# A feed-forward stage whose first unit is done by plain products instead of seven block products

## The chip, the cores and the metric

The kernel runs on one core of one Trainium2 chip. What counts is the time of one execution in microseconds on the device. All times below are of that kind, and "us" is a microsecond. TensorE (PE in the profile) multiplies matrices, PEld is its loading of weights, VectorE (DVE), ScalarE (ACT) and GpSimd (POOL) work on tiles of 128 partitions, and SyncE (SP) issues most transfers. Each engine takes its instructions in the order of its own queue.

## The reference, cut to what matters

The network has three layers over 512 tokens of width 1024. The first has attention, a recurrent part and one feed-forward part, the other two have a feed-forward part, a mix of four attentions, and another feed-forward part. So there are five feed-forward stages, f0 to f4 below, in order of time. The first layer adds the whole product, the others half of it:

```python
def rms_norm(x, g):
    y = xf * lax.rsqrt(jnp.mean(xf * xf, axis=-1, keepdims=True) + EPS)
    return (y * g.astype(jnp.float32)).astype(x.dtype)

def swiglu(h, w_gate, w_up, w_down):
    return (jax.nn.silu(h @ w_gate) * (h @ w_up)) @ w_down
...
        x = x + 0.5 * swiglu(rms_norm(x, ffn1_norm[l]), ffn1_w_gate[l], ffn1_w_up[l], ffn1_w_down[l])
        h = rms_norm(x, mix_norm[l])
...
        x = x + 0.5 * swiglu(rms_norm(x, ffn2_norm[l]), ffn2_w_gate[l], ffn2_w_up[l], ffn2_w_down[l])
        x = rms_norm(x, final_norm[l])
```

The hidden width is 2816, eleven units of 256 gate and 256 up columns.

## The kernel before

Activations stand transposed: xT is 8 tiles (k) of 128 features by 512 tokens. Every fp32 operand is split into a high part and the rest (hi and lo, xh and xl, wh and wl), and every product is three matmuls: hi by hi, hi by lo, lo by hi. `feat` and `feat2` (L144 to L165) do this plainly, with weights that `stream` (L116) loads in two buffers ("raw") and splits (L133 on ScalarE, L135 on VectorE or GpSimd).

A unit of a feed-forward stage isn't done so. Its gate and up columns and the two halves of the tokens make a 2 by 2 scheme of blocks over even and odd k tiles, which takes seven products of sums of blocks instead of eight (`unit`, L620; `prod`, L584). A product is 24 matmuls of 128x256, so a unit has 168. The block sums of the weights are called factors. A0 to A3 are the four blocks of a unit's weights, loaded by `load` (L575). s1 = A2 + A3 is added by a transfer that GpSimd issues (L625), s2 and s4 by VectorE (L628, L660), s3 by ScalarE and a transfer (L626, L627). `prod` splits a factor into wh (ScalarE, L588) and wl (VectorE, L593, or ScalarE and a transfer, L590 and L591). The block sums of x are made once a stage by `combine` (L378): x is the scaled tile, t its differences, and the splits by L219 and L220 go to xh, xl, x3h and x3l. The first products of unit 0 need A0 and s1.

The norm's sum of squares runs beside it. For each k tile `norm_sq` (L227) squares on ScalarE (L231) and adds on GpSimd (L233) into acc; ahead of f3 `final_norm` (L735) adds two such sums, one on VectorE (L752), one on GpSimd (L762). Then `norm_r` reduces acc on TensorE (L203), VectorE makes nm (L194), GpSimd the power (L196), TensorE spreads it (L212), and ScalarE copies it to rB (L215). rB scales a unit's results after the products (`act`, L610); the products don't need it. At f3 eight scalings of xT follow (L780).

After the last product of a unit L668 adds it into c, then come SiLU, the multiply by up, a split into fh and fl, and every two units a share of the down product (`down`, L672), whose matmuls are plain ones of 128x512 (L150 to L152). Later units' products and these are laced together.

A scheduler puts the instructions in order ahead of time. Each has its place in the program as its priority, and `tc.high_priority(offset=n)` moves it n instructions ahead. Before, a factor and its split stand 3000 ahead and a load 6000, which is more than a unit's instructions, so those of units 0 and 1 stand ahead of the stage as far as buffers allow. A1 lies in the "raw" buffers, which live throughout; A0, A2 and A3 lie in the pool of the stage (`ph_f`), whose memory held other tiles before, so their loads wait for the last use of those. In unit 0 the first three products are cut in two ranges of k (L629), so that they can begin before the last pair of tiles is there.

Of the kernel before, what the change touches and what calls it, by code (L numbers as in the profile page):

```python
# [8 lines left out]
FT = mybir.dt.float32  # L9
# [9 lines left out]
T = 512  # L19
# [73 lines left out]
class Kern:  # L93
# [284 lines left out]
    def combine(self, k, xk, g, xc):  # L378
# [3 lines left out]
        p = k // 2  # L382
        if k % 2 == 0:
            xc["x"] = self.t4("x")
            if "hi" not in xc:
                xc["hi"], xc["lo"] = ((self.xp.tile([128, 4, 4, 256], FR, tag="x" + n, name="x" + n),
                                       self.x3.tile([128, 4, 3, 256], FR, tag="x3" + n, name="x3" + n)) for n in "hl")
        x = xc["x"]
        hi, lo = xc["hi"], xc["lo"]
        S.activation(x[:, 2 * (k % 2):2 * (k % 2) + 2], xk.rearrange("p (a b) -> p a b", a=2), AF.Copy, scale=g)  # L390
        if k % 2 == 0:
            self.split(hi[0][:, p, 0], lo[0][:, p, 0], x[:, 0])
            return
        self.split(hi[0][:, p, 1:3], lo[0][:, p, 1:3], x[:, 2:4])
# [5 lines left out]
        self.split(hi[0][:, p, 3], lo[0][:, p, 3], t[:, 0])  # L400
        self.split(hi[1][:, p], lo[1][:, p], t[:, 1:4])

    def norm_c(self, gname, g0):
# [3 lines left out]
        def tile_done(k):  # L407
            self.combine(k, xT[:, k], self.col(gname, g0 + k), xc)
            self.norm_sq(xT[:, k], k, acc)
# [146 lines left out]
    def ffn(self, f, half, norm):  # L556
# [6 lines left out]
        with tc.tile_pool(name="ph_f", bufs=1) as pf:  # L563
            self.pf = pf
            self.t4 = lambda n: pf.tile([128, 4, 256], FT, tag="c", name=n, bufs=3)
            xh, xl = ([lambda p, c=c, x=x: x[c // 4][:, p, c % 4] for c in range(7)] for x in self.xc)
# [4 lines left out]
            def load(u, i):  # L571
                pool, tag, n = (pf, "raw2", 3) if i % 3 == 0 else (pf, "S", 4) if i == 2 else (self.wp, "raw", 2)
                t = pool.tile([128, 2 * T], FT, tag=tag, name=f"A{i}", bufs=n)
                with tc.high_priority(offset=6000):
                    nc.sync.dma_start(t, I["w_gu"][f, u, i])  # L575
# [5 lines left out]
            def early():  # L581
                return tc.high_priority(offset=3000)

            def prod(x, c, ranges=((0, 4),), dma=False):  # L584

                h, o = (pf.tile([128, 2 * T], FR, tag=n, name=n, bufs=3) for n in ("wh", "wl"))
                with tc.high_priority(offset=3000):
# [8 lines left out]
                for a, b in ranges:  # L596
                    for i in range(2):
                        out = ps[:, i * 256:i * 256 + 256]
                        for p in range(a, b):
                            sl = slice((4 * i + p) * 128, (4 * i + p) * 128 + 128)  # L600
                            mm(out, h[:, sl], xh[c](p), start=i == 0 and p == 0, stop=False)  # L601
                            mm(out, h[:, sl], xl[c](p), start=False, stop=False)  # L602
                            mm(out, o[:, sl], xh[c](p), start=False, stop=i == 1 and p == 3)  # L603
                    yield
                return ps.rearrange("p (a b) -> p a b", a=2)

            def act(u, j, c):

                k = 2 * u + j
                V.tensor_mul(c, c, rT)  # L610
# [6 lines left out]
            def soon():  # L617
                return tc.high_priority(offset=1000)

            def unit(u):  # L620
# [8 lines left out]
                r = ((0, 3), (3, 4)) if u == 0 else ((0, 4),)  # L629
                heads = [prod(x, c, r) for x, c in ((a11, 0), (s1, 3), (s2, 4))]  # L630
                c1, c2 = (pf.tile([128, 2, 2, 256], FT, tag="c", name="c", bufs=3) for _ in range(2))
                if u == 0:
                    for g in heads:
                        next(g)
                ps = whole(heads[0])
# [3 lines left out]
                ps = whole(heads[1])  # L639
# [3 lines left out]
                ps = whole(heads[2])  # L643
# [4 lines left out]
                ps = whole(prod(a12, 1, dma=True))  # L648
# [3 lines left out]
                ps = whole(prod(s3, 5))  # L652
# [8 lines left out]
                ps = whole(prod(s4, 2))  # L661
# [4 lines left out]
                ps = whole(prod(a22, 6, dma=True))  # L666
# [40 lines left out]
            for u in range(11):  # L707
                if u % 2 == 0 and u:
# [26 lines left out]
    def final_norm(self, l):  # L735
# [11 lines left out]
        def tile_done(k):  # L747
# [13 lines left out]
            if k:  # L761
                G.tensor_tensor(acc2[0], acc2[0], sq, op=OP.add)  # L762
# [1241 lines left out]
```

## Time and profile before

| | |
|---|---|
| median of 3 runs | 3338.43 us (3334.64 to 3338.55) |
| profiled execution: its time | 3331.87 us |
| profiled execution: its span | 3330.1 us |
| mean granted clock of TensorE | 0.949 of full |
| busy: TensorE, VectorE, ScalarE, GpSimd | 91%, 67%, 53%, 39% of the span |

The span runs from the first to the last instruction of the profiled execution; its own time is 1.8 us longer. Shares are of the span. An engine that is busy nine tenths of the time over the whole can still stand idle in short stretches, so stretches are looked at one by one.

### The profile page before, as it was taken

The page shows a single profiled execution, that of the slowest core. Times are in us where ns is not written, and L with a number is a line of the kernel's source. Part 1 is how long each engine was busy: PE and PEld are TensorE (multiplying, and loading weights), DVE is VectorE, ACT ScalarE, POOL GpSimd, SP SyncE. Part 2 cuts the span into 40 slices and gives each one's busy share as a digit, 9 for nine tenths or more (in the row PEclk, how much of TensorE's full clock was granted, in tenths as well). Part 3 has the DMA queues.
Part 4 walks back from the last instruction along what each step waited for, and adds up shares of the span by engine and source line. Part 5 has one row for each costly group of instructions (what it writes and reads, how often), then busy time and mean ns, then how long its engine had stood idle before and what let it go on. Part 6 is the DMA issues. An engine that isn't in the chain of part 4 may idle for free. (4 is left out here: it accounts for less than half of the span.)

```text
span 3330.1 us, 50223 instructions
## 1 busy us (share of the span) xinstructions
PE 3020.4 (91%) x19249; PEld 2721.9 (82%) x19249; DVE 2216.2 (67%) x3447; ACT 1764.0 (53%) x3007; POOL 1291.1 (39%) x1139
## 2 busy tenths in 40 slices
PE   7999999979997899999895999958999998859998
PEld 6888778878996899998774899948999987658997
DVE  7577774566765667658675766666766578667665
ACT  4577773454544454457654545444544667545453
POOL 0466531122332323277732332223322877233322
PEclk9999999989998999999897999979999999979999
DMA  4311113466763766532213766436664321157662
GB/s 131 106 58 50 50 39 102 141 164 156 177 152 86 177 165 163 132 101 91 57 32 79 173 161 164 111 98 168 167 164 109 106 83 51 32 133 170 172 162 73
DMA packets 136984, 391.74 MB, mean 118 GB/s; under 512 B 30692, under 2 KB 40420, under 8 KB 136584
## 3 DMA queue, kind: packets, MB, share of 16 engines
q1 hardware_dynamic: 105064, 273.18, 26.5%
q0 software_dynamic: 31680, 115.36, 19.0%
q8 instruction: 151, 2.47, 0.3%
q14 instruction: 89, 0.73, 0.1%
HBM read 297.77 MB, written 6.80 MB: 91 GB/s over the span
## 5 line engine op out<-in xcount | busy, mean ns | idle before, releaser
L133 ACT ACTIVATE hi<-raw 128x512 fp32r<-128x512 f32 (+3 forms) x512 | 314.5, 620 | 470.1 <-PE ps_t L151 187.3
L135 DVE TENSOR_TENSOR lo<-raw,hi 128x512 fp32r<-128x512 f32 (+1 forms) x342 | 295.5, 868 | 156.4 <-ACT hi L133 152.4
L588 ACT ACTIVATE wh<-A 128x1024 fp32r<-128x1024 f32 x220 | 231.5, 1055 | 311.2 <-PE ps_mm L602 146.7
L591 POOL DMA_DIRECT2D wl<-A x110 | 97.7, 888 | 693.9 <-ACT wl L590 664.2
L151 PE MATMUL ps_t<-fl,hi 128*128 128x512 f32 x760 | 297.3, 391 | 0.0
L152 PE MATMUL ps_t<-fh,lo 128*128 128x512 f32 x760 | 295.7, 389 | 0.0
L150 PE MATMUL ps_t<-fh,hi 128*128 128x512 f32 x760 | 295.5, 393 | 0.0
L601 PE MATMUL ps_mm<-xh,wh 128*128 128x256 f32 x920 | 268.8, 292 | 28.6 <-ACT wh L588 28.6
L603 PE MATMUL ps_mm<-xh,wl 128*128 128x256 f32 x920 | 270.6, 294 | 26.1 <-DMA wl<-A 16.3
L601 PE MATMUL ps_s<-xh,wh 128*128 128x256 f32 x840 | 244.6, 291 | 25.5 <-ACT wh L588 25.5
L602 PE MATMUL ps_mm<-xl,wh 128*128 128x256 f32 x920 | 267.4, 291 | 0.0
L603 PE MATMUL ps_s<-xh,wl 128*128 128x256 f32 x840 | 246.4, 293 | 17.8 <-DMA wl<-A 12.3
L181 PE MATMUL ps_mm<-lo,xh 128*128 128x256 f32 (+1 forms) x896 | 257.6, 290 | 2.0 <-DVE lo L135 2.0
L182 PE MATMUL ps_mm<-hi,xl 128*128 128x256 f32 (+1 forms) x896 | 255.5, 288 | 4.1 <-DVE xl L238 4.1
L135 POOL TENSOR_TENSOR lo<-raw,hi 128x512 fp32r<-128x512 f32 (+2 forms) x170 | 231.9, 1372 | 65.3 <-ACT hi L133 61.3
L180 PE MATMUL ps_mm<-hi,xh 128*128 128x256 f32 (+1 forms) x896 | 256.1, 290 | 0.1
L612 POOL TENSOR_TENSOR c<-c 128x512 f32<-128x512 f32 x110 | 164.8, 1498 | 212.6 <-ACT c L611 212.5
L593 DVE TENSOR_TENSOR wl<-S,wh 128x1024 fp32r<-128x1024 f32 x165 | 208.8, 1266 | 55.9 <-ACT wh L588 55.4
L602 PE MATMUL ps_s<-xl,wh 128*128 128x256 f32 x840 | 243.6, 290 | 0.0
L588 ACT ACTIVATE wh<-S 128x1024 fp32r<-128x1024 f32 x165 | 174.2, 1056 | 73.3 <-PE ps_mm L602 40.8
L603 PE MATMUL ps_s<-x3h,wl 128*128 128x256 f32 x720 | 207.1, 288 | 6.4 <-DMA wl<-A 6.1
L601 PEld LDWEIGHTS ps_mm<-xh,wh 128*128 128x128 f32 x920 | 184.1, 200 | 32.7 <-ACT wh L588 30.5
(580 smaller groups left out, 9908.5 us busy)
## 6 DMA issues: line engine op xcount, KB each, us to landing
A<-in_w_gu SPq DMA_DIRECT2D x220, 512.0 KB
wl<-A POOLq DMA_DIRECT2D x110, 512.0 KB, 5.4
raw<-in_w_d SPq DMA_DIRECT2D x108, 512.0 KB
S<-in_w_gu POOLq DMA_DIRECT2D x55, 512.0 KB, 7.4
A<-A POOLq DMA_DIRECT2D x55, 512.0 KB, 4.6
raw<-in_w_o SPq DMA_DIRECT2D x24, 512.0 KB
raw<-in_w_c SPq DMA_DIRECT2D x16, 512.0 KB
raw<-in_w_m SPq DMA_DIRECT2D x16, 512.0 KB
```

The source lines that it names most:

```text
L133: nc.scalar.activation(hi[:, :c], x, AF.Copy)
L135: eng.tensor_tensor(lo[:, :c], x, hi[:, :c].bitcast(FT), op=OP.subtract)
L150: mm(ps, wh, mh(km), start=s, stop=False)
L151: mm(ps, wh, ml(km), start=False, stop=False)
L152: mm(ps, wl, mh(km), start=False, stop=e)
L180: mm(out[tb], h, wh, start=k == 0 and tb % 2 == 0, stop=False)
L181: mm(out[tb], h, wl, start=False, stop=False)
L182: mm(out[tb], o, wh, start=False, stop=k == K - 1 and tb % 2 == 1)
L588: S.activation(h, x, AF.Copy)
L601: mm(out, h[:, sl], xh[c](p), start=i == 0 and p == 0, stop=False)
L602: mm(out, h[:, sl], xl[c](p), start=False, stop=False)
L603: mm(out, o[:, sl], xh[c](p), start=False, stop=i == 1 and p == 3)
```

## The change

Five things change. Unit 0 of each stage is done by `first`: plain products of 8 k tiles, 2 column tiles, gate and up, three matmuls each, 96 matmuls of 128x512, from weights w_g0 and w_u0 that `stream` loads and splits; L631 multiplies each result by rB on leaving the accumulator. For it `combine` splits each xT tile as a whole (`norm_split`, L237 and L238), and the block sums keep four tiles t of their own, split in one go of 1024 columns. Factors and loads are moved ahead by `ahead` and twice that, which begins at 113 instructions for unit 1 and grows with the place in the stage up to 3000. The adds of squares in `norm_c` and the second sum of `final_norm` go from GpSimd to VectorE. And the tiles of x grow, for which the memory of GpSimd's transfer queue is set to 4096 bytes; the mix's boxes lie in the larger tile.

```diff
@@ -380,25 +380,23 @@
 
         V, S = self.nc.vector, self.nc.scalar
         p = k // 2
+        if not xc:
+            xc["hi"], xc["lo"] = ((self.xp.tile([128, 8, T], FR, tag="x" + n, name="x" + n),
+                                   self.x3.tile([128, 4, 4, 256], FR, tag="x3" + n, name="x3" + n)) for n in "hl")
         if k % 2 == 0:
             xc["x"] = self.t4("x")
-            if "hi" not in xc:
-                xc["hi"], xc["lo"] = ((self.xp.tile([128, 4, 4, 256], FR, tag="x" + n, name="x" + n),
-                                       self.x3.tile([128, 4, 3, 256], FR, tag="x3" + n, name="x3" + n)) for n in "hl")
         x = xc["x"]
         hi, lo = xc["hi"], xc["lo"]
+        self.norm_split(xk, k, g, hi[0], lo[0])
         S.activation(x[:, 2 * (k % 2):2 * (k % 2) + 2], xk.rearrange("p (a b) -> p a b", a=2), AF.Copy, scale=g)
         if k % 2 == 0:
-            self.split(hi[0][:, p, 0], lo[0][:, p, 0], x[:, 0])
             return
-        self.split(hi[0][:, p, 1:3], lo[0][:, p, 1:3], x[:, 2:4])
         t = self.t4("t")
         V.tensor_sub(t[:, 0], x[:, 1], x[:, 0])
         V.tensor_sub(t[:, 1], x[:, 3], t[:, 0])
         V.tensor_sub(t[:, 2], x[:, 3], x[:, 1])
         V.tensor_sub(t[:, 3], x[:, 2], t[:, 1])
-        self.split(hi[0][:, p, 3], lo[0][:, p, 3], t[:, 0])
-        self.split(hi[1][:, p], lo[1][:, p], t[:, 1:4])
+        self.split(hi[1][:, p], lo[1][:, p], t)
 
     def norm_c(self, gname, g0):
 
@@ -406,7 +404,7 @@
 
         def tile_done(k):
             self.combine(k, xT[:, k], self.col(gname, g0 + k), xc)
-            self.norm_sq(xT[:, k], k, acc)
+            self.norm_sq(xT[:, k], k, acc, self.nc.vector)
 
         def finish():
             self.xc = xc["hi"], xc["lo"]
@@ -563,7 +561,12 @@
         with tc.tile_pool(name="ph_f", bufs=1) as pf:
             self.pf = pf
             self.t4 = lambda n: pf.tile([128, 4, 256], FT, tag="c", name=n, bufs=3)
-            xh, xl = ([lambda p, c=c, x=x: x[c // 4][:, p, c % 4] for c in range(7)] for x in self.xc)
+            xs = [x[0] for x in self.xc]
+            xh, xl = ([lambda p, x=x: x[0][:, 2 * p, :256], lambda p, x=x: x[0][:, 2 * p + 1, :256],
+                       lambda p, x=x: x[0][:, 2 * p + 1, 256:]]
+                      + [lambda p, c=c, x=x: x[1][:, p, c] for c in range(4)] for x in self.xc)
+            ks = [(k, k) for k in range(8)]
+            ahead = [3000]
             rT = rB.rearrange("p (t b) -> p t b", t=2)[:, :, None, :].to_broadcast([128, 2, 2, 256])
             fh, fl = {}, {}
             nbank = [0]
@@ -571,7 +574,7 @@
             def load(u, i):
                 pool, tag, n = (pf, "raw2", 3) if i % 3 == 0 else (pf, "S", 4) if i == 2 else (self.wp, "raw", 2)
                 t = pool.tile([128, 2 * T], FT, tag=tag, name=f"A{i}", bufs=n)
-                with tc.high_priority(offset=6000):
+                with tc.high_priority(offset=2 * ahead[0]):
                     nc.sync.dma_start(t, I["w_gu"][f, u, i])
                 return t
 
@@ -579,12 +582,12 @@
                 return pf.tile([128, 2 * T], FT, tag="S", name="S", bufs=4)
 
             def early():
-                return tc.high_priority(offset=3000)
-
-            def prod(x, c, ranges=((0, 4),), dma=False):
+                return tc.high_priority(offset=ahead[0])
+
+            def prod(x, c, dma=False):
...
             def act(u, j, c):
 
                 k = 2 * u + j
-                V.tensor_mul(c, c, rT)
+                if u:
+                    V.tensor_mul(c, c, rT)
                 S.activation(c[:, :, 0], c[:, :, 0], AF.Silu)
                 G.tensor_tensor(c[:, :, 0], c[:, :, 0], c[:, :, 1], op=OP.mult)
                 h, o = (pf.tile([128, T], FR, tag=n, name=n, bufs=8) for n in ("fh", "fl"))
@@ -616,6 +618,19 @@
 
             def soon():
                 return tc.high_priority(offset=1000)
+
+            def ctile():
+                return pf.tile([128, 2, 2, 256], FT, tag="c", name="c", bufs=3)
+
+            def first():
+
+                c = [ctile() for _ in range(2)]
+                for i, n in enumerate(("w_g0", "w_u0")):
+                    ps = self.feat2(self.stream(I[n][f], 8, 256), ks, lambda k: xs[0][:, k], lambda k: xs[1][:, k])
+                    for m in range(2):
+                        V.tensor_mul(c[m][:, :, i], *(x.rearrange("p (a b) -> p a b", a=2) for x in (ps[m], rB)))
+                for m in range(2):
+                    act(0, m, c[m])
 
             def unit(u):
...
-                r = ((0, 3), (3, 4)) if u == 0 else ((0, 4),)
-                heads = [prod(x, c, r) for x, c in ((a11, 0), (s1, 3), (s2, 4))]
-                c1, c2 = (pf.tile([128, 2, 2, 256], FT, tag="c", name="c", bufs=3) for _ in range(2))
-                if u == 0:
-                    for g in heads:
-                        next(g)
-                ps = whole(heads[0])
+                c1, c2 = ctile(), ctile()
+                ps = prod(a11, 0)
                 with soon():
                     S.copy(c1[:, 0], ps)
                 yield
-                ps = whole(heads[1])
+                ps = prod(s1, 3)
...
             d = iter(())
-            for u in range(11):
-                if u % 2 == 0 and u:
+            first()
+            at = 130
+            for u in range(1, 11):
+                ahead[0] = min(3000, at * 7 // 8)
+                at += 215 if u == 1 else 330
+                if u % 2 == 0:
                     d = down(list(range(2 * u - 4, 2 * u + (0 if u < 10 else 2))), u == 10)
                 for i, _ in enumerate(unit(u)):
                     if i in ((2, 6) if u < 10 else (2,)):
...
             if k:
-                G.tensor_tensor(acc2[0], acc2[0], sq, op=OP.add)
+                V.tensor_add(acc2[0], acc2[0], sq)
...
-        x3 = [self.x3.tile([128, 6, T], FT, tag=n, name="box3") for n in ("x3h", "x3l")]
-        slots = {"P": [x3[0][:, i] for i in range(6)] + [x3[1][:, i] for i in range(2)],
+        x3 = [self.x3.tile([128, 8, T], FT, tag=n, name="box3") for n in ("x3h", "x3l")]
+        slots = {"P": [x3[0][:, i] for i in range(8)],
...
+    A["w_g0"], A["w_u0"] = (np.stack([blocks(f[i][:, :256], 256)[0] for f in ff]) for i in range(2))
...
-    nc = bacc.Bacc("TRN2", target_bir_lowering=False, num_devices=1)
+    nc = bacc.Bacc("TRN2", target_bir_lowering=False, num_devices=1, dynamic_dma_scratch_size=4096)
```

Three places show how the queues change, all at the start of f2. Rows are an instruction's line, what it does, tiles written and read, and shape. First TensorE before: the last plain matmuls of the mix (ps_mm from yhl), the reduction of acc, and unit 0's first product (xh by A0's wh).

```order
L150 MATMUL ps_mm<-yhl,hi 128x512
L151 MATMUL ps_mm<-yhl,hi 128x512
L152 MATMUL ps_mm<-yhl,lo 128x512
L203 MATMUL ps_n<-ones,acc 128x1 x4
L212 MATMUL ps_n<-ident,rt 128x128 x4
L601 MATMUL ps_s<-xh,wh 128x256
L602 MATMUL ps_s<-xl,wh 128x256
L603 MATMUL ps_s<-xh,wl 128x256
```

The same after, at the end of the 96 plain matmuls (xh and xl by hi and lo of w_g0 into ps_s and of w_u0 into ps_t), which begin straight behind the mix's last matmul. L603 to L605 are now unit 1's first product.

```order
L150 MATMUL ps_t<-xh,hi 128x512
L151 MATMUL ps_t<-xl,hi 128x512
L152 MATMUL ps_t<-xh,lo 128x512
L203 MATMUL ps_n<-ones,acc 128x1 x4
L212 MATMUL ps_n<-ident,rt 128x128 x4
L603 MATMUL ps_s<-xh,wh 128x256
L604 MATMUL ps_s<-xl,wh 128x256
L605 MATMUL ps_s<-xh,wl 128x256
```

So the reduction and all products moved behind the plain unit; in f0 and f1 the reduction stands after 42 of the 96. Next the loads on SyncE before, from the last weights of the mix on: A1 of units 0 and 1, then A0, A2, A3 of unit 0 and A0 of unit 1.

```order
L126 DMA raw<-in_w_o 128x1024 x7
L575 DMA A_18249<-in_w_gu 128x1024
L575 DMA A_18495<-in_w_gu 128x1024
L575 DMA A_18145<-in_w_gu 128x1024
L575 DMA A_18147<-in_w_gu 128x1024
L575 DMA A_18149<-in_w_gu 128x1024
L575 DMA A_18391<-in_w_gu 128x1024
```

And after: the plain unit's weights, A1 of unit 1, a first piece of the down weights, A1 of unit 2, and only then A0 (A_18103), A2 and A3 of unit 1.

```order
L126 DMA raw<-in_w_o 128x1024 x7
L126 DMA raw<-in_w_g 128x1024 x2
L126 DMA raw<-in_w_u 128x1024 x2
L578 DMA A_18207<-in_w_gu 128x1024
L126 DMA raw<-in_w_d 128x1024
L578 DMA A_18491<-in_w_gu 128x1024
L578 DMA A_18103<-in_w_gu 128x1024
L578 DMA A_18105<-in_w_gu 128x1024
L578 DMA A_18107<-in_w_gu 128x1024
```

Seven transfers now stand between the mix's weights and the load of A0 (the four of the plain unit among them) where two of A1 stood. Last VectorE after, at the end of the block sums: acc is the sum of squares, t and x3l the block sums and their split, nm the step that waits for L203, and L631 empties the plain unit.

```order
L233 TENSOR_TENSOR acc<-acc,sq 128x512
L135 TENSOR_TENSOR lo<-raw,hi 128x512
L398 TENSOR_TENSOR t<-x,t 128x256
L220 TENSOR_TENSOR x3l<-t,x3h 128x1024
L194 TENSOR_SCALAR nm<-ps_n 128x4
L220 TENSOR_TENSOR x3l<-t,x3h 128x1024
L631 TENSOR_TENSOR c<-ps_s,rB 128x2x256 x2
L631 TENSOR_TENSOR c<-ps_t,rB 128x2x256 x2
L596 TENSOR_TENSOR wl<-A_18103,wh 128x1024
```

Before, the last two x3l stood behind nm too, no L233 stood in this queue, and A0's split into wl followed at once.

## Rows read from the trace of the kernel before

**Rows 1.** The profile's page, part 1: engine, busy us (share of the span), instructions.
```profile
PE 3020.4 (91%) x19249; PEld 2721.9 (82%) x19249; DVE 2216.2 (67%) x3447; ACT 1764.0 (53%) x3007; POOL 1291.1 (39%) x1139
```

**Rows 2.** Windows ahead of f0, f2, sum of five: length, busy (count), clock.
```profile
667.00:679.30 12.30, 4.16 (x18) 3.57 (x17) 6.39 (x12) 5.47 (x10) 3.60 (x3) 0.63 0.28 108
...
1773.30:1806.60 33.30, 4.20 (x18) 3.59 (x17) 22.95 (x42) 16.41 (x31) 16.78 (x8) 0.54 0.12 39
...
sum 137.20, PE 24.74 PEld 21.48 DVE 91.04 ACT 62.92 POOL 53.64; mean PE 4.95 PEld 4.30 DVE 18.21 ACT 12.58 POOL 10.73
```

**Rows 3.** The waits in total: engine, line, released by; us, times, longest.
```profile
PE ps_n L203 <- POOL acc L233: 56.9, 4, 22.2
```

**Rows 4.** Timeline of TensorE at f2: start, us, line, tiles; idle before it.
```profile
1795.73 1.86 PE L203 MATMUL ps_n<-ones,acc 128*128 128x1 f32 x8 [22.21 <-POOL acc L233]
...
1806.57 0.58 PE L601 MATMUL ps_s<-xh,wh 128*128 128x256 f32 x1 [5.44 <-ACT wh L588]
```

**Rows 5.** Timeline of all engines at f2's start.
```profile
1776.91 2.69 POOL L233 TENSOR_TENSOR acc<-acc,sq 128x512 f32<-128x512 f32 x2 [0.72 <-ACT sq L231]
1777.00 1.48 DVE L220 TENSOR_TENSOR xl<-x,xh 128x256 fp32r<-128x256 f32 x1
...
1785.90 0.41 DVE L220 TENSOR_TENSOR xl<-t,xh 128x256 fp32r<-128x256 f32 x1
...
1800.57 0.96 DVE L220 TENSOR_TENSOR x3l<-t,x3h 128x768 fp32r<-128x768 f32 x1 [0.91 <-ACT x3h L219]
1801.16 0.59 ACT L215 COPY rB<-ps_n 128x512 f32<-128x512 f32 x1 [0.62 <-PE ps_n L212]
1801.61 1.75 SPq L575 DMA_DIRECT2D A<-in_w_gu  x4
```

**Rows 6.** Windows from unit 0's last L668 to unit 1's (f0, f2, f3, sum).
```profile
714.40:747.20 32.80, 28.47 (x204) 26.67 (x203) 22.24 (x22) 17.55 (x24) 10.81 (x9) 0.95 0.69 162
...
1847.70:1873.90 26.20, 22.86 (x167) 22.15 (x167) 17.09 (x19) 13.55 (x19) 8.66 (x9) 0.93 0.68 153
2252.80:2286.90 34.10, 28.65 (x204) 27.65 (x204) 21.90 (x22) 17.75 (x24) 10.74 (x9) 0.90 0.63 158
...
sum 141.60, PE 125.43 PEld 120.08 DVE 98.49 ACT 74.69 POOL 48.05; mean PE 25.09 PEld 24.02 DVE 19.70 ACT 14.94 POOL 9.61
```

**Rows 7.** Timeline of TensorE: 128x512 matmuls at full, then half clock.
```profile
1399.73 0.39 PE L150 MATMUL ps_t<-fh,hi 128*128 128x512 f32 x1
1399.96 0.39 PE L151 MATMUL ps_t<-fl,hi 128*128 128x512 f32 x1
...
1771.37 0.63 PE L150 MATMUL ps_mm<-yhl,hi 128*128 128x512 f32 x1
1771.80 0.63 PE L151 MATMUL ps_mm<-yhl,hi 128*128 128x512 f32 x1
```

**Rows 8.** Lines L238 and L233: durations min/median/max ns, first and last start.
```profile
L238 DVE SCALAR_TENSOR_TENSOR xl<-xT,cols,xh x16: 742/1410/1784, 1433.2 to 2595.3; 128x512 fp32r<-128x512 f32 x16
...
L233 POOL TENSOR_TENSOR acc<-acc,sq x42: 1261/1370/7467, 637.4 to 2930.3; 128x512 f32<-128x512 f32 x42
...
L233 DVE TENSOR_TENSOR acc<-acc,sq x7: 677/680/686, 11.0 to 20.8; 128x512 f32<-128x512 f32 x7
```

**Rows 9.** f3: TensorE's L203, and L575's loads between 2178 and 2283 us.
```profile
2196.24 1.87 PE L203 MATMUL ps_n<-ones,acc 128*128 128x1 f32 x8 [17.33 <-DVE acc L752]
...
L575 SPq DMA_DIRECT2D A<-in_w_gu x12: 327/328/516, 2213.2 to 2281.1; - x12
```

**Rows 10.** Windows of nine units of f0, and of the first mix stage.
```profile
768.00:1051.00 283.00, 280.97 (x1887) 260.19 (x1886) 195.66 (x221) 139.14 (x184) 85.01 (x68) 1.00 0.59 146
1400.00:1773.00 373.00, 344.91 (x2153) 304.42 (x2152) 248.85 (x484) 219.88 (x468) 225.46 (x209) 0.94 0.24 68
```

**Rows 11.** The page, part 6: GpSimd's transfers, KB, us from issue to landing.
```profile
wl<-A POOLq DMA_DIRECT2D x110, 512.0 KB, 5.4
```

More of the change, by code (lines that the diff above doesn't have):

```diff
@@ L581, in early @@
             def early():
-                return tc.high_priority(offset=3000)
-            def prod(x, c, ranges=((0, 4),), dma=False):
+                return tc.high_priority(offset=ahead[0])
+            def prod(x, c, dma=False):
                 h, o = (pf.tile([128, 2 * T], FR, tag=n, name=n, bufs=3) for n in ("wh", "wl"))
-                with tc.high_priority(offset=3000):
+                with early():
                     S.activation(h, x, AF.Copy)
@@ L595, in prod @@
                 ps = self.bank(("mm", "s")[nbank[0] % 2])
[L596 to L604, printed above, removed]
+                for i in range(2):
+                    out = ps[:, i * 256:i * 256 + 256]
+                    for p in range(4):
+                        sl = slice((4 * i + p) * 128, (4 * i + p) * 128 + 128)
+                        mm(out, h[:, sl], xh[c](p), start=i == 0 and p == 0, stop=False)
+                        mm(out, h[:, sl], xl[c](p), start=False, stop=False)
+                        mm(out, o[:, sl], xh[c](p), start=False, stop=i == 1 and p == 3)
                 return ps.rearrange("p (a b) -> p a b", a=2)
@@ L642, in unit @@
                 yield
-                ps = whole(heads[2])
+                ps = prod(s2, 4)
                 with soon():
@@ L647, in unit @@
                 a12 = load(u, 1)
-                ps = whole(prod(a12, 1, dma=True))
+                ps = prod(a12, 1, dma=True)
                 with soon():
@@ L651, in unit @@
                 yield
-                ps = whole(prod(s3, 5))
+                ps = prod(s3, 5)
                 with soon():
@@ L660, in unit @@
                     V.tensor_sub(s4, a12, s2)
-                ps = whole(prod(s4, 2))
+                ps = prod(s4, 2)
                 with soon():
@@ L665, in unit @@
                 yield
-                ps = whole(prod(a22, 6, dma=True))
+                ps = prod(a22, 6, dma=True)
                 with soon():
```

## The prediction

> **What bounds the kernel now.** I read the busy table first. TensorE is busy 91% of the 3330.1 us span [rows 1], so only a stretch in which it stands still has time to give. There are five such stretches, one ahead of each feed-forward stage (f0 to f4, in order of time). Cut into windows that run from the last plain matmul ahead of a stage to the first product of its unit 0 [rows 2], they are 137 us long together, from 12.3 us in f0 to 33 us and more in f2 to f4, and TensorE works 24.7 us of them. Its granted clock there is 0.63 in f0 and 0.54 in f2, so most of a window lies at the lower of its two levels (1.2 of 2.4 GHz). The list of waits gives the first reason: four times the reduction L203 waits for the adds of squares on GpSimd, 56.9 us in all [rows 3]. The timeline of f2 shows the queue [rows 4]: L203 starts 22.21 us after TensorE fell idle, L212 behind it, and the products behind both, as TensorE takes its instructions in order. But the sum is not the only late thing. In [rows 5] the last split into x3l starts at 1800.57; at 1801.61 the first load of A0 is issued, since the stage's buffers lie where earlier work ended only then; and the first product starts at 1806.57, five us after the issue. So two chains end together, and what the change is worth hangs on the second: when A0 is issued, and what follows it.
>
> What follows is slow too. I take as the end of a unit the add L668 that empties its last product: in f2 unit 0 ends at 1847.7, 46.1 us after A0's issue at 1801.6. From there to unit 1's end it takes 32.8 us in f0, 26.2 in f2, 34.1 in f3, and 141.6 us in the five stages together [rows 6].
>
> **The change, part by part.** *Unit 0 by plain products.* Seven products of 24 matmuls of 128x256 go, with their factors; 96 matmuls of 128x512 come. One of these follows the other by 0.23 us at full clock and 0.43 us at half [rows 7], so the new unit is 96 x 0.23 = 22 us, or 41 us at half clock. It needs no A0, only x and its own weights, which the load queue now has ahead of the stage's other loads. So it fills the wait in which TensorE stood. Unit 1 becomes the first unit that needs A0, and goes through what unit 0 goes through now: it ends as long after A0's issue as unit 0 did (f2: 46.1 us). If A0 is issued as before, unit 1 ends where unit 0 ended, and each stage gains the stretch between the two ends. That is the first term: **141.6 us**. The 22 us are no cost as long as they lie in that wait. In f0 and f3 the stretch holds 204 matmuls and not the 168 of one unit [rows 6], so 36/204 of 32.8 and of 34.1 us is other units' work, still to be done: **minus 11.8 us**.
>
> *A0's issue.* It waits for the last x3l (in f3 for the eight scalings L780). VectorE gains eight L238 splits of 0.74 us and seven adds of 0.68 us [rows 8], 10.7 us a stage. It loses the twelve small splits of x, some 6 us by the 0.41 us of a piece of 256 columns [rows 5], and its last splits grow from 768 to 1024 columns, some 1.2 us by width from 0.96 us. Net 5.9 us. GpSimd's adds go, and with them contention: such an add took 7467 ns once against 1261 at best [rows 8], and a split of 0.41 us took 1.48 us when an add ran beside it [rows 5]. That gives perhaps 4 us back in f2. More important is where things stand in the queue. In f2 and f4 the last x3l stands behind nm (L194) on VectorE, before and after; nm waits for L203, and TensorE now does that behind all 96 plain matmuls. By hand, the splits, adds and weight splits take VectorE to about 25 us behind the stage's start before the last add, the plain unit ends near there, and A0 goes out some 3 us later: about 4 us later than now, in both. In f3 A0 came 17 us after L203's start (2196.24 to 2213.2 us [rows 9]); L203 now follows a plain unit of 22 us that waits in part for the last k tiles, so about 26 us instead of 17.5, and A0 some 8.6 us later. In f1 I take 3 us, in f0 1 us, where L203 stands in the middle of the plain unit. Together **minus 20.6 us**. Bounds: 0 if the contention that goes pays for it all; 66 us if the plain unit runs at half clock in f2 to f4 (41 us, so 20 to 15 us more in each, 45 in all).
>
> A rule of the Trainium skill bears on this term ("SBUF — State Buffer", "Who interferes with whom"): a VectorE instruction with two SBUF inputs and a GpSimd instruction that reads SBUF exclude each other, and whichever issues first holds the port. By it, nothing contends at a stage's start any more, and the term would be nearer 10 than 20 us; the 1.48 us beside the 0.41 us agree. I keep 20, since the queue order decides in three of the stages.
>
> *New waits.* The four L631 that empty the plain unit (0.68 us each by the add in [rows 8]) need rB, which comes some 6 us after L203's start [rows 4, 5]. They stand on VectorE ahead of the split of A0's weights; the first product starts five us after A0's issue, so at most 2.7 us, in practice 1 to 2 us a stage: **minus 7 us**. Bounds 0 and 14. Behind them wait the third matmul of the first product, and SiLU of unit 0, which nobody needs before the first down product.
>
> *Smaller lead of the loads* (`ahead`). Later units take 31.4 us each (283 us for nine, TensorE busy 280.97 of it [rows 10]); with 168 products and a share of the down product they are full. The new lead is one unit's instructions at the start and 3000 at the end, so a factor is still made a unit ahead: nothing, unless a load comes late, bound 1 us a unit. *The mix stages.* Their code is the same, but the order inside differs: 281 of the 1991 rows on TensorE stand elsewhere. TensorE idles 28 us in the first of them [rows 10]. I take 0, bounds plus and minus 12.
>
> **Sum.** 141.6 - 11.8 - 20.6 - 7 = 102 us. The profiled execution took 3331.87 us (1.8 us beyond its span), so 3229.7; the median of the three runs is 6.6 us above it, which makes **3236 us**.
>
> **Rivals.** (a) *Half clock.* In f2 to f4 the plain unit is fed k tile by k tile, one each 2 to 3 us, while its gate half needs 6 x 0.23 = 1.4 us for a tile. If the clock stays at 1.2 GHz through it, it takes 41 us, ends near 42 us instead of 25, and L203, x3l and A0 come that much later: 45 us lost, about 3281 us. For it speaks that the clock falls in these windows now [rows 2]; against it, that plain work follows the matmuls before it with hardly a gap and is dense once the up half joins. The Trainium skill ("TensorE: Matmul & The Clock Gate", "HAM oscillation — how this bites in real kernels") says that an engine fed in bursts with waits between them is throttled anew each time. By that rule this rival would be the likelier; the trace shows falls only where TensorE did nothing at all.
> (b) *More than that.* The waits between unit 0's products now vanish as well, because the factors of unit 1 are made while the plain unit and early down products run: 130 us, 3208 us. Against it: A2 and A3 are issued behind A0 in the same breath.
> (c) *No gain.* A0 slips as far as unit 0 grew, 20 to 28 us a stage: 3338 us. VectorE is busy 23 of 33 us in f2 [rows 2], so the net 5.9 us can't do this alone; it takes (a) and late weights of the up half together.
> (d) *Slower.* The change cuts the scratch memory of GpSimd's transfers to 4096 bytes. If that holds only one transfer, each of the four that GpSimd issues for a unit waits for the one before: 4 x 5.4 us [rows 11] = 21.6 us of waiting a unit, against 0.61 x 31.4 = 19.2 us in which GpSimd idles now [rows 1, 10]. The excess of 2.4 us in 50 units is 120 us, and late factors would add to it: 3236 + 120 = 3356 us or more. It decides as soon as fewer than two transfers fit. The trace shows transfers in flight together now, but not how many fit.
>
> **Chances and range.** Forecast (3205 to 3262) 0.6; (a) 0.16; (b) 0.07; (c) 0.06; (d) 0.07; a mix stage that goes awry by more than its idle time 0.04. The measurement can tell about 0.2%, 6.7 us, from no change. Faster by more than that: 0.6 + 0.16 + 0.07 and some of (c), 0.86; same 0.05; slower 0.09. The range of 8 in 10 takes in the low bound of the terms (141.6 - 11.8 = 130 us, and 12 from the mix: 3196) and (a) with the mix against it: 3196 to 3290.
>
> **What would show it.** Right: the five windows hold plain matmuls from the first us on, L203 waits under 3 us, A0 goes out at about 8, 18, 32, 43 and 32 us behind the last matmul of the stage before, and unit 1 ends 40 to 47 us after that. Wrong, and how: a granted clock near 0.5 through the plain unit of f2 to f4 (a); no idle time of TensorE in unit 1 (b); A0 later by 20 us (c); GpSimd's issues L594 and L640 of some 5 us in place of 0.9 (d); or units 2 to 10 that take over 32 us each, if the smaller lead is too small.

## The result, and the profile after

The changed kernel takes 3194.36 us (median of four runs, 3184.8 to 3197.1) against 3336.53 us before on the same chips: a ratio of 0.957, with a 95% interval of 0.955 to 0.959. That is 142 us less. The forecast was 3236 us, 100 us less, in a range from 3196 to 3290 us: the direction and the mechanism came true, the size was 42 us too small, and the time lies 1.6 us under the range.

The profiled execution has a span of 3194.8 us. Its page, part 1, answers to [rows 1]:

```profile
PE 2989.7 (94%) x18889; PEld 2676.2 (84%) x18889; DVE 2164.0 (68%) x3452; ACT 1734.7 (54%) x2967; POOL 1190.6 (37%) x1074
```

TensorE is busy 30.7 us less and idle about 105 us less. So most of the gain is time in which it stood. The windows of the five plain units, from the last plain matmul ahead of a stage to the last of its 96, answer to [rows 2] (f0, f2, f3 and the sum of five; columns as there):

```profile
667.60:691.20 23.60, 23.60 (x113) 19.80 (x112) 12.22 (x20) 11.90 (x17) 2.97 (x3) 1.00 0.66 189
...
1723.00:1748.60 25.60, 23.15 (x97) 17.62 (x96) 25.36 (x47) 18.68 (x31) 0.00 (x0) 1.00 0.20 62
2098.60:2122.10 23.50, 22.33 (x97) 17.86 (x96) 22.97 (x40) 17.97 (x29) 0.00 (x0) 1.00 0.31 92
...
sum 124.90, PE 116.03 PEld 92.74 DVE 106.42 ACT 82.72 POOL 5.44; mean PE 23.21 PEld 18.55 DVE 21.28 ACT 16.54 POOL 1.09
```

Where TensorE worked 24.7 of 137 us, it now works 116 of 125, at the full clock. The plain units end 23.5 to 27.2 us behind a stage's start; 22 was their work, 25 the forecast for f2. The timeline of f2 after answers to [rows 4, 5]:

```profile
1747.87 0.69 DVE L233 TENSOR_TENSOR acc<-acc,sq 128x512 f32<-128x512 f32 x1
...
1748.87 0.94 PE L203 MATMUL ps_n<-ones,acc 128*128 128x1 f32 x8
1749.19 4.48 SPq L578 DMA_DIRECT2D A<-in_w_gu  x5
...
1750.62 1.22 DVE L220 TENSOR_TENSOR x3l<-t,x3h 128x1024 fp32r<-128x1024 f32 x1
...
1754.80 0.59 ACT L215 COPY rB<-ps_n 128x512 f32<-128x512 f32 x1 [4.21 <-PE ps_n L212]
...
1755.72 1.06 ACT L591 ACTIVATE wh<-A 128x1024 fp32r<-128x1024 f32 x1 [0.34 <-DMA A<-in_w_gu]
...
1756.83 0.58 PE L603 MATMUL ps_s<-xh,wh 128*128 128x256 f32 x1 [2.07 <-ACT wh L591]
```

The stage starts at 1723.0. The last sum ends with the plain unit, at 25.6 us, and L203 has no wait of note in front of it. The last x3l ends at 28.8 us, and the load of A0 goes out there (the first of the five merged issues is the second A1, A0 follows at 28.9). The first block product starts at 33.8 us; before it was unit 0's at 33.4. So in f2 the block products begin when they began, one unit further on.

### The profile page after: what moved, and what is told of

It reads as the page before. It is cut to its first block, busy times and chain, and to the rows that moved or that the text cites. A ratio compares the mean times of both kernels' runs of the same rounds, so it can differ in the third digit from the quotient of the medians.

```text
span 3194.8 us, 49346 instructions
## 1 busy us (share of the span) xinstructions
PE 2989.7 (94%) x18889; PEld 2676.2 (84%) x18889; DVE 2164.0 (68%) x3452; ACT 1734.7 (54%) x2967; POOL 1190.6 (37%) x1074
## 5 line engine op out<-in xcount | busy, mean ns | idle before, releaser
L133 ACT ACTIVATE hi<-raw 128x512 fp32r<-128x512 f32 (+1 forms) x552 | 338.5, 620 | 466.5 <-PE ps_t L151 184.4
L135 DVE TENSOR_TENSOR lo<-raw,hi 128x512 fp32r<-128x512 f32 (+1 forms) x382 | 324.1, 853 | 163.9 <-ACT hi L133 159.5
L603 PE MATMUL ps_mm<-x3h,wh 128*128 128x256 f32 x800 | 228.4, 285 | 13.2 <-ACT wh L591 13.2
L605 PE MATMUL ps_mm<-x3h,wl 128*128 128x256 f32 x800 | 228.4, 285 | 4.2 <-DVE wl L596 2.5
L605 PE MATMUL ps_s<-x3h,wl 128*128 128x256 f32 x800 | 226.5, 283 | 4.2 <-DMA wl<-A 4.2
L603 PE MATMUL ps_s<-x3h,wh 128*128 128x256 f32 x800 | 226.7, 283 | 2.4 <-ACT wh L591 2.4
L604 PE MATMUL ps_mm<-x3l,wh 128*128 128x256 f32 x800 | 227.8, 285 | 0.0
L604 PE MATMUL ps_s<-x3l,wh 128*128 128x256 f32 x800 | 226.3, 283 | 0.0
L605 PE MATMUL ps_s<-xh,wl 128*128 128x256 f32 x600 | 178.0, 297 | 25.1 <-DMA wl<-A 22.4
L603 PE MATMUL ps_s<-xh,wh 128*128 128x256 f32 x600 | 176.1, 293 | 16.6 <-ACT wh L591 16.6
L605 PE MATMUL ps_mm<-xh,wl 128*128 128x256 f32 x600 | 171.7, 286 | 15.7 <-DMA wl<-A 11.6
```

The source lines that it names most:

```text
L133: nc.scalar.activation(hi[:, :c], x, AF.Copy)
L135: eng.tensor_tensor(lo[:, :c], x, hi[:, :c].bitcast(FT), op=OP.subtract)
```

## Experiments

Two lengths are read from every profile. A feed-forward stage runs from the last plain matmul ahead of it to the add that ends its last unit (L668 before, its counterpart after); a mix stage runs from there to the last plain matmul ahead of f2 or f4. Sums of the five stages and of the two mixes, in us, with the ratio of the runs to the kernel before:

| kernel | five stages | two mixes | ratio, 95% interval |
|---|---|---|---|
| before | 1871.4 | 354.9 + 345.7 | 1 |
| changed | 1752.4 | 342.9 + 340.4 | 0.957 (0.955 to 0.959) |
| e1 sums on GpSimd | 1753.9 | 340.9 + 337.7 | 0.959 (0.957 to 0.961) |
| e2 sums alone | 1852.4 | 353.8 + 353.2 | 0.997 (0.995 to 0.998) |
| e3 old lead | 1741.0 | 343.3 + 341.4 | 0.956 (0.954 to 0.958) |
| e4 two plain units | 1671.8 | 354.6 + 348.2 | 0.941 (0.940 to 0.943) |
| e5 old boxes | 1746.1 | 340.5 + 342.1 | 0.957 (0.955 to 0.958) |
| e6 new boxes alone | 1864.8 | 350.0 + 347.3 | 0.999 (0.998 to 1.000) |
| e7 final rB elsewhere | 1730.5 | 342.1 + 339.4 | 0.953 (0.951 to 0.954) |
| e8 two plain units, final rB | 1659.7 | 354.8 + 354.9 | 0.939 (0.938 to 0.941) |
| e9 changed, again | 1743.8 | 343.2 + 340.0 | 0.957 (0.955 to 0.959) |
| e10 plain unit alone | 1752.5 | 343.2 + 338.4 | 0.960 (0.957 to 0.962) |
| e11 two plain units, GpSimd | 1667.0 | 354.9 + 351.4 | 0.940 (0.938 to 0.942) |
| e12 three plain units | 1672.5 | 343.9 + 341.0 | 0.934 (0.932 to 0.937) |
| e13 changed, other turn | 1746.4 | 351.6 + 351.8 | 0.962 (0.960 to 0.964) |
| e14 two plain units, other turn | 1662.0 | 346.0 + 340.1 | 0.931 (0.929 to 0.933) |
| e15 before, other turn | 1876.5 | 344.1 + 337.2 | 0.994 (0.992 to 0.996) |

The changed kernel's stages differ by 8.6 us between its two profiles, so differences of that size in the second column say nothing.

### The parts of the change (e1, e2, e3, e10)

e1, the changed kernel with

```diff
-            self.norm_sq(xT[:, k], k, acc, self.nc.vector)
+            self.norm_sq(xT[:, k], k, acc)
...
-                V.tensor_add(acc2[0], acc2[0], sq)
+                G.tensor_tensor(acc2[0], acc2[0], sq, op=OP.add)
```

> The changed kernel with the adds of squares (norm_c's and the second sum of final_norm) back on GpSimd. Theory P (the plain unit does the work: it fills the wait in which TensorE stood, so the reduction L203 may come as late as the plain unit's end): the adds of 1.3 us each end about 22 us behind a stage's start in f2 and f4, the plain unit ends at 25, so nothing waits for them; contention costs VectorE up to 4 us a stage. 3194 to 3210 us. Rival S (the sums on VectorE carry a good part of the gain, by the 56.9 us that L203 waited before): 3194 + 57 = about 3250 us.

Measured 3193.12 us, ratio 0.959, a microsecond under theory P's range and far from S. The plain unit hides the sums on either engine. They aren't free on GpSimd. The window of f2's plain unit in e1:

```profile
1712.00:1743.10 31.10, 25.28 (x106) 19.28 (x105) 30.77 (x44) 19.53 (x32) 12.45 (x8) 0.95 0.16 51
```

It is 31.1 us long and not 25.6, with VectorE busy almost throughout for fewer instructions (44, not 47), while GpSimd works 12.45 us beside it. A0 goes out at 9.6, 19.5, 31.6, 41.5 and 31.6 us in the five stages, against 8.6, 17.6, 28.9, 39.1 and 28.3 in the changed kernel. The five stages together are only 1.5 us longer; what makes up for the rest was not followed.

e2, the kernel before with the reverse edit and nothing else:

> The kernel before with nothing changed but the adds of squares, now on VectorE. Theory P: L203 comes a few us earlier or not at all, since VectorE has 4.8 us more to do per stage, and the load of A0 still goes out behind the last x3l; so within 15 us of before, 3322 to 3350 us. Rival S: the wait of 56.9 us goes, 3280 us.

Measured 3318.09 us beside 3328.95 of before on that chip, 10.9 us less: within the 15 us of theory P, far from S. (It is 4 us under the 3322 of the forecast, as before itself was lower on that chip.) f2 in e2:

```profile
1785.49 1.84 PE L203 MATMUL ps_n<-ones,acc 128*128 128x1 f32 x8 [20.18 <-DVE acc L233]
1785.59 1.96 DVE L220 TENSOR_TENSOR x3l<-t,x3h 128x768 fp32r<-128x768 f32 x2
1787.62 1.75 SPq L575 DMA_DIRECT2D A<-in_w_gu  x4
...
1792.55 0.58 PE L601 MATMUL ps_s<-xh,wh 128*128 128x256 f32 x1 [1.71 <-ACT wh L588]
```

TensorE's wait for the sum is 20.18 us where it was 22.21: moving the adds didn't remove it. But A0 goes out 22.7 us behind the stage's start and not 28.5, and f2 is 7.2 us shorter. Over the five stages the gain is 19.0 us, while the mixes take 6.4 us more. What P had not foreseen is that A0 would come earlier.

e3, `ahead[0] = 3000` in place of `min(3000, at * 7 // 8)`:

> The changed kernel with the lead of the factors and loads fixed at 3000 and 6000 instructions, as before. Theory P: buffers, not the lead, decide when A0 can be loaded, and the order of the loads hardly differs, so the time is that of the changed kernel within 0.3%, 3185 to 3204 us. Rival L (the smaller lead keeps factors of unit 1 out of the way of the plain unit, and is a good part of the gain): 3215 us or more.

Measured 3181.33 us, ratio 0.956. That is 4 us under theory P's range and far from L: the smaller lead is no part of the gain. e10 is e1 and e3 in one:

> The plain unit alone: the changed kernel with the adds of squares back on GpSimd and the lead of factors and loads as before (the larger tiles of x and the smaller transfer memory stay, as the plain unit needs them). Theory P: the plain unit is the whole gain of the stages, 119 us, so ratio 0.956 to 0.963, 3185 to 3210 us. Rival S: one of the two other parts is needed with it, since sums on GpSimd and old lead together delay A0: above 3225 us.

Measured 3194.93 us, ratio 0.960: theory P. The stages gain 118.9 us, as much as with all the parts; the mixes take 19.0 us less, which is another matter (below). e9 is the changed kernel unaltered:

> The changed kernel once more, unaltered, beside the next three, since kernels that hardly differ from it gave ratios from 0.956 to 0.959. Theory O (the order of the mix and the state of the runs move the time by some us, the stages don't): ratio 0.955 to 0.959; mix stages within 4 us of 342.9 and 340.4; the five feed-forward stages together within 10 us of what they took in its first profile.

Measured 3185.73 us, ratio 0.957: theory O, with the mixes within 0.4 us and the stages 8.6 us below those of the first profile.

### More of the same (e4, e12), and the load of A0 (e7, e8, e11)

e4, besides arrays w_g0 and w_u0 that hold two units:

```diff
-            first()
-            at = 130
-            for u in range(1, 11):
+            for u in range(2):
+                first(u)
+            at = 260
+            for u in range(2, 11):
...
-                at += 215 if u == 1 else 330
+                at += 330
```

> The changed kernel with the first two units of each stage by plain products (w_g0 and w_u0 hold two units, the block products begin with unit 2). Theory P: a second plain unit fills what TensorE still waits in unit 1. In the first 100 us of a stage it stands or goes at half clock for 16 us in f0 and some 29 to 35 in f2 to f4 by the pace of its matmuls; A0 comes at about 28 us, its first two products are ready at 44 us, and two plain units end at 47 us. So up to 15 us a stage in f1 to f4 and 8 in f0, less 1.6 us a stage for the dearer unit: 3194 - 60 = about 3135 us. Rival B (the start of the block products costs its waits wherever it stands, since their factors come one by one): no gain, and 5 x 1.6 us more, 3194 to 3205 us.

Measured 3135.82 us, ratio 0.941. Theory P is right in kind, and it is right to the microsecond by luck: the stages take 80.6 us less (72.0 against the second profile of the changed kernel), not 60, and the mixes 19.5 us more, of which P said nothing. The first 100 us of f2, in the changed kernel and then in e4 (columns as in [rows 2]):

```profile
1723.00:1823.00 100.00, 80.78 (x486) 71.87 (x485) 75.34 (x96) 53.86 (x74) 24.55 (x20) 0.91 0.59 152
```

```profile
1704.80:1804.80 100.00, 93.99 (x523) 80.57 (x522) 75.61 (x106) 57.58 (x83) 20.74 (x18) 0.99 0.60 159
```

A second plain unit takes TensorE from 81 to 94 us of work and its clock from 0.91 to 0.99. e12 is e8 below with a third, laced with the first down products:

> Three plain units and the spread factor in its own buffer. Theory P: with two the loads of A0 and its first products are ready before the plain work ends (A0 at 9 to 33 us, plain end at 45 to 56 us), so a third has only the small waits of unit 2 to fill, at 1.6 us a stage more: 3118 to 3140 us, no clear gain over two. Rival B (block products lose time wherever they begin, so each plain unit more gains as the second did): about 3128 - 50 = 3080 us.

Measured 3111.05 us, between the two and in neither's range. In the stages P is right that there is no gain: 1672.5 us against 1659.7 with two (e8). The gain came in the mixes, 684.9 us against 709.7, of which neither theory spoke.

e7, in `final_norm`:

```diff
-            rB = self.bcast(rf, self.pf, "raw2", 3)
+            rB = self.bcast(rf, self.tp, "sq", 2)
```

> The changed kernel with the spread factor of the final scalings in a small buffer of its own in place of one of the stage's load buffers, so that in f3 the load of A0 waits only for the last split of x and not for the eight scalings L794. Theory A (a stage's loss hangs on when A0 is issued): in f3 A0 goes out at 27 to 30 us in place of 39.1, unit 1's end comes that much earlier, and the kernel gains 8 to 11 us in that stage. Rival R (the scalings themselves hold VectorE, and A0's split into wl stands behind them in its queue): A0 lands earlier, but the first product starts within 3 us of where it did, and nothing is gained.

Measured 3174.32 us, ratio 0.953. The first block product of f3 in the changed kernel, and then f3 in e7:

```profile
2142.55 0.58 PE L603 MATMUL ps_s<-xh,wh 128*128 128x256 f32 x1 [10.96 <-ACT wh L591]
```

```profile
2117.15 1.92 PE L212 MATMUL ps_n<-ident,rt 128*128 128x128 f32 x8 [2.10 <-DVE rt L786]
2118.94 1.06 ACT L591 ACTIVATE wh<-A 128x1024 fp32r<-128x1024 f32 x1 [7.04 <-DMA A<-in_w_gu]
...
2123.39 0.58 PE L603 MATMUL ps_s<-xh,wh 128*128 128x256 f32 x1
2124.26 6.71 DVE L794 SCALAR_TENSOR_TENSOR xT<-xT,cols,sq 128x512 f32<-128x512 f32 x8 [0.33 <-ACT sq L215]
```

A0 went out at 26.1 us and not 39.1, the first block product started at 34.3 and not 43.9, ahead of the scalings. That is theory A against R: what counts is when A0 can be loaded. But the stage is 6.6 us shorter and not 8 to 11, and the rest of what e7 gains on the changed kernel lies in other stages, where it changes nothing. e8 and e11 put this together with two plain units, e11 with the sums on GpSimd too:

> Two plain units and the spread factor of the final scalings in its own buffer. With two plain units f3 lost 24.9 us against the pace of its matmuls and the others 5 to 12, with A0 at 45.7 us. Theory A: A0 out by 36 us, f3's loss near 13 us, so 3135 - 11 = about 3125 us, if the mix stages keep their 354.6 and 348.2 us. Rival R: as two plain units alone, 3131 to 3140 us.

Measured 3128.53 us, ratio 0.939; A0 in f3 goes out at 33.4 us, and f3 is 9.3 us shorter than in e4. Theory A, by f3; the kernel's time lies between the two.

> Two plain units, the spread factor of the final scalings in its own buffer, and the adds of squares on GpSimd. Theory P: behind two plain units of 47 us the sums are hidden on either engine, so as with them on VectorE within 0.4% in the stages; the mix stages may fall out otherwise by up to 15 us each, by the order that the scheduler finds. 3105 to 3140 us. Rival S: contention with GpSimd's adds delays the splits that feed the plain unit, 3145 us or more.

Measured 3131.02 us, ratio 0.940: theory P, though the stages are 0.44% longer than in e8, just over its 0.4%.

### The mixes (e5, e6, e13, e14, e15)

The two mixes gave 17.3 us of the gain with code that only had its boxes moved. Windows of both, before and then in the changed kernel:

```profile
1418.30:1773.10 354.80, 326.71 (x2027) 287.40 (x2026) 242.79 (x476) 215.45 (x462) 220.72 (x205) 0.94 0.23 67
2563.80:2909.50 345.70, 316.12 (x2028) 278.54 (x2026) 243.35 (x473) 215.43 (x463) 220.07 (x206) 0.97 0.24 69
```

```profile
1380.20:1723.00 342.80, 316.95 (x2027) 279.00 (x2026) 238.77 (x479) 217.06 (x464) 216.41 (x205) 0.97 0.24 71
2457.00:2797.40 340.40, 317.30 (x2028) 280.27 (x2028) 238.89 (x476) 216.64 (x466) 218.30 (x205) 0.96 0.24 72
```

The same 2027 matmuls keep TensorE busy 9.8 us less in the first mix, at a mean clock of 0.97 in place of 0.94. In the second the clock is no better, and it idles 6.5 us less. e5 takes back the boxes in the changed kernel, e6 (with the transfer memory of 4096 bytes) moves them in the one before:

```diff
-        slots = {"P": [x3[0][:, i] for i in range(8)],
+        slots = {"P": [x3[0][:, i] for i in range(6)] + [x3[1][:, i] for i in range(2)],
```

> The changed kernel with the mix's boxes P back in two tiles (six and two). The mix stages took 354.9 and 345.7 us before and 342.9 and 340.4 after, 17.3 us less, though their code is the same but for these boxes. Theory O (the order that the scheduler finds for the mix makes the difference; this kernel's order there is nearly that of the changed kernel): mix stages within 4 us of 342.9 and 340.4, time as the changed kernel's within 0.3%. Rival T (the boxes' tiles make it, since a box shared a tile with others that are written at other times): mix stages back at 354.9 and 345.7, 17 us more.

> The kernel before with only the mix's boxes P in one tile of eight, and GpSimd's transfer memory at 4096 bytes. Theory O (order): its order in the mix is nearly that of before, so the mix stages take 354.9 and 345.7 us within 4 us and the time is that of before within 0.3%. Rival T (tiles): mix stages of 343 and 340 us, 17 us less than before. The smaller transfer memory by itself: nothing by the theory; 120 us or more if it held one transfer only.

Measured 3189.04 us and ratio 0.957 for e5; 3327.57 us and 0.999 for e6, whose mixes are these:

```profile
1420.10:1770.10 350.00, 319.58 (x2027) 281.22 (x2026) 243.16 (x477) 215.68 (x463) 220.41 (x206) 0.96 0.23 68
2555.90:2903.20 347.30, 320.22 (x2027) 282.05 (x2026) 243.66 (x473) 215.01 (x463) 219.45 (x206) 0.96 0.23 69
```

The first is 4.9 us shorter than before, a little more than theory O allowed, though TensorE, ScalarE and GpSimd go through it in the same order as before. So a single mix says little within 5 us. The boxes are not the cause, and the smaller transfer memory costs nothing.

By then the mixes took 338 to 344 us in every kernel with 10 or 8 block units a stage, and 346 to 355 us with 11 or 9. A stage's products take the accumulator tags "mm" and "s" by turns, so an odd number of units ends on the other tag. e13 (changed kernel), e14 (e8) and e15 (before) alter that alone:

```diff
-            nbank = [0]
+            nbank = [1]
```

> The changed kernel with the turn of the two accumulator tags begun on the other one, so that a stage's last product ends on s as before, and nothing else. Theory K (that turn sets which of two orders the scheduler finds for the mix): the mix stages take 348 to 355 us each as before, and the kernel 10 to 20 us more than the changed one, ratio 0.960 to 0.964. Rival C (the mix orders differ by chance, and any edit may give either): mix stages of 343 and 340 us, ratio 0.956 to 0.958.

> Two plain units, spread factor in its own buffer (ratio 0.9391, mix stages 354.8 and 354.9 us), and the turn of the accumulator tags begun on the other one, so that it ends on mm. Theory K: mix stages 338 to 344 us, the kernel about 25 us faster, ratio 0.931 to 0.934. Rival C: no gain, 0.938 to 0.940.

> The kernel before with the turn of the accumulator tags begun on the other one, and nothing else of the change. Theory K: mix stages 338 to 344 us in place of 354.9 and 345.7, ratio 0.993 to 0.996, so that about 17 us of the change's gain are to be had without it. Rival C: ratio 0.999 to 1.001.

Measured 3209.0 us (0.962), 3103.67 us (0.931) and 3313.11 us (0.994). Windows of the mixes in e13, then e14, then e15:

```profile
1370.70:1722.30 351.60, 322.63 (x2028) 284.95 (x2027) 243.32 (x479) 216.90 (x464) 219.75 (x205) 0.94 0.23 70
2459.20:2811.00 351.80, 321.13 (x2027) 282.57 (x2026) 244.71 (x474) 216.56 (x464) 220.06 (x205) 0.96 0.23 70
```

```profile
1349.10:1695.10 346.00, 319.08 (x2028) 282.42 (x2027) 241.52 (x479) 217.23 (x465) 219.35 (x205) 0.95 0.23 71
2389.80:2729.80 340.00, 317.84 (x2027) 281.37 (x2026) 238.70 (x474) 215.94 (x464) 218.07 (x205) 0.95 0.24 72
```

```profile
1420.60:1764.70 344.10, 319.88 (x2028) 282.74 (x2026) 240.52 (x477) 214.70 (x463) 216.90 (x206) 0.95 0.23 70
2554.10:2891.30 337.20, 315.11 (x2028) 279.31 (x2026) 236.58 (x472) 214.76 (x462) 215.61 (x206) 0.96 0.24 71
```

All three moved as theory K said: the two mixes take 20.1 us more in e13 than in the changed kernel, 23.6 less in e14 than in e8, and 19.3 less in e15 than before, though e14's first lies 2 us above its forecast and e15's second 0.8 below. Over all kernels they take 679 to 686 us with one turn and 697 to 710 with the other.

So some 20 us hang on the turn of the tags. But it doesn't pick between two orders: read from every trace, TensorE's order in the first mix comes in four forms with one turn and in five with the other. The turn came with the change by accident, as a stage now has ten block units and not eleven; with the old turn (e13) the change gives 127 us, 3209.0 beside 3335.7. By which step the turn costs the time (an order or the tag itself, which matmul waits, and where the clock falls) was not taken apart. e14 is the fastest kernel of the study.

## Why the prediction was right and where it was wrong

**The mechanism was right.** TensorE stood waiting ahead of each stage, and the plain unit fills that wait. The block products begin when they began, within 1.2 us, in f2 and f4 alone; in f3 they begin 4.5 us later, in f1 7.6 and in f0 16. L203's wait on GpSimd [rows 3] is gone; what is left of waits for acc is this, from the list of waits after:

```profile
PE ps_n L203 <- DVE acc L766: 2.3, 1, 2.3
```

The first term, 141.6 us between the ends of unit 0 and unit 1 [rows 6], stood; the deductions from it were too large, and the mixes were left out. The mixes are what took the time out of the range: with the tags' turn as before, the same change takes 3209.0 us, inside it (e13).

**Step "A0's issue", minus 20.6 us: mis-sized, it measured 8.9.** A0 goes out 1.2 us later than before in f0, 2.5 in f1, 0.4 in f2, 4.5 in f3 and 0.3 in f4. In f2 and f4 the chain by hand was right (last add at 25 us in f2, plain end near it, A0 three us later), but it gave A0 at 28 us, and I then wrote 4 us of delay, which is 32 us: 7.3 of the 11.7 us too much are this slip. In f3 L203 came at 23.8 us and not at 26, and A0 15.3 us behind it and not 17: 4.1 us more. The adds' place counts too. GpSimd is idle in the plain units of f2 and f3, and the adds on VectorE take 680 to 694 ns each; with the adds on GpSimd (e1) the same sum of delays is 20.2 us. The prediction weighed a rule of the Trainium skill here ("SBUF — State Buffer", "Who interferes with whom"): a VectorE instruction with two SBUF inputs and a GpSimd instruction that reads SBUF shut each other out. By it the term would have been nearer 10, and the trace agrees with 8.9; I set it aside for a queue order that I had added up wrongly.

**Steps "other units' work" and "new waits", minus 18.8 us: measured minus 13.7, in other places.** In f2 to f4 unit 1 ends 40.6, 39.1 and 43.2 us after A0's issue, near the 40 to 47 of the forecast; unit 0 took 46.1, 39.6 and 47.2 before. The first block product follows A0's issue by 4.9, 4.9 and 5.6 us there, and by 5.0, 4.9 and 4.7 before, so the new wait behind L631 is 0.9 us at most. In f0 and f1 unit 1 takes 54.7 and 50.6 us where unit 0 took 40.1 and 44.8, since TensorE comes to the block products only behind the plain unit, at 27 to 29 us, while A0 is out at 8.6 and 17.6. The product of s1, whose factor is later than A0, is the first in f0 and the second in f1, and there TensorE still waits, 6.05 us in f1, and in f0 so:

```profile
695.21 1.06 ACT L591 ACTIVATE wh<-A 128x1024 fp32r<-128x1024 f32 x1 [0.76 <-DMA A<-A]
...
696.32 0.58 PE L603 MATMUL ps_mm<-x3h,wh 128*128 128x256 f32 x1 [4.72 <-ACT wh L591]
...
699.37 0.58 PE L605 MATMUL ps_mm<-x3h,wl 128*128 128x256 f32 x1 [2.25 <-DVE wl L596]
```

That makes 10.4 us over the five stages; 3.3 more are lost in the units behind. The stages together gain 141.6 - 8.9 - 13.7 = 119.0 us, 17 more than forecast.

**Step "the mix stages", 0 with bounds of 12: wrong, it gave 17.3 us.** That rows move in the order was seen, but not that the turn of the tags moves two stages of 350 us by some 20 us in sum (e13 to e15). The 17.3 us are 5 us outside the bounds. The rest, 0.8 us, is lost ahead of f0: 119.0 + 17.3 - 0.8 = 135.5 us, the difference of the spans to 0.2.

**The step from the profile to the median.** I added 6.6 us, as before's profiled execution lay that far under its median. After, it took 3197.1 us and lies 2.7 us above its own. So 9.3 us more are nobody's mechanism, only two single executions.

**The rivals.** (a) fell: the granted clock was 1.00 in the plain units of f2 and f3, whose gaps were 1.2 us at most. The Trainium skill's rule that a TensorE fed in bursts falls back ("TensorE: Matmul & The Clock Gate", "HAM oscillation — how this bites in real kernels") found no case there. But the reading that the clock falls only where TensorE did nothing at all doesn't hold. In the first mix of the kernel before it fell in ten microseconds of which TensorE worked 7.90, and stayed at the lower level, 0.50, through ten of which it worked 9.19:

```profile
1588.30:1598.30 10.00, 7.90 (x50) 6.96 (x49) 5.98 (x19) 5.97 (x15) 7.63 (x11) 0.84 0.25 61
1598.30:1608.30 10.00, 9.19 (x42) 8.21 (x40) 8.02 (x14) 5.84 (x14) 9.65 (x7) 0.50 0.08 24
```

(b) fell as told: the waits in unit 1 went on, and only a second plain unit took most of them away (e4). (c) fell with A0's delay of 8.9 us. (d) fell: GpSimd issues a wl transfer in 881 ns, 888 before, and e6 has the small memory at no cost. The smaller lead cost nothing (e3).

## What to carry to other kernels

When an engine waits at the start of a stage for prepared operands, look for work of that stage that needs none of them, even if it is a little dearer: 96 plain matmuls of 22 us in place of 20 us' worth of block products bought 24 us a stage, and a second such unit some 15 more. A third showed none in the stages; by the forecast of e12 that is because the operands are then ready before the cheap work is done, which no run tested further. And time the parts that you didn't change: here a change of parity in an accumulator's turn gave 17 us that looked like part of the gain.

## What was not expected of the hardware

- TensorE's clock held through gaps that I had feared: in f1 it waited 3.29 us for the first tiles of x, and the mean granted clock from the stage's start to the plain unit's end was 1.00. In the mixes it fell amid work.
- The same 2027 matmuls of a mix keep TensorE busy between 315 and 327 us, at mean clocks of 0.94 to 0.97. The turn of the accumulator's tags moves this, but isn't all of it: before and in e6 TensorE has the same order in the first mix, and is busy 326.71 and 319.58 us.
- Sums that VectorE does itself cost it less than having GpSimd do them beside it: f2's plain unit ended at 25.6 us with seven adds more on VectorE, and at 31.1 us without them, though the kernel's time was the same (ratios of 0.957 and 0.959).
